# A row softmax on one core: the third tile loaded in eight DMAs of every eighth partition, and the split row of the second tile made whole

## The chip, the core and the metric

The kernel runs on one core of a Trainium2 chip. The core has five engines with their own instruction streams: TensorE (PE), VectorE (DVE), ScalarE (ACT), GpSimd (POOL) and SyncE (SP). Data moves between the chip's main memory (HBM) and the on-chip memory (SBUF, 128 partitions) in DMAs. A DMA is issued by SP, ACT or POOL into a queue of that engine, and is carried out in packets by the core's 16 DMA engines. Each DMA counts a semaphore up by 16 when it has landed, one by each DMA engine.

The metric is the device time of one execution in microseconds (us). Three runs of the kernel before gave 160.0, 160.11 and 161.32 us; the median is 160.11 us.

## The reference

```python
def setup_inputs():
    batch, seq, dim = 16, 1024, 512
    return {"x": np.random.randn(batch, seq, dim).astype(np.float32)}

def reference(x):
    x_scaled = x / 2.0
    x_max = np.max(x_scaled, axis=-1, keepdims=True)
    exp_x = np.exp(x_scaled - x_max)
    return (exp_x / np.sum(exp_x, axis=-1, keepdims=True)).astype(np.float32)
```

That is 16,384 rows of 512 fp32 values: 33.55 MB in, 33.55 MB out.

## The kernel before, in words

The 16,384 rows are laid out as 128 rows for each of the 128 partitions, 2 KB each. They are cut into ten tiles (`TILES`, L10): tile 0 has 3 rows per partition, tile 1 has 5, and tiles 2 to 9 have 15 each. In HBM the rows of one partition in one tile stand one behind the other, so a 15-row tile is 128 runs of 30,720 bytes. The tiles live in one array, `arena`, of 98 rows per partition; tiles 8 and 9 reuse the places of tiles 0 to 3 (`LATE`, L14).

**Loads.** `load` (L113) issues one DMA for a tile. For tile 1 (`SPREAD`, L20) it issues three: the first four rows of all partitions, the fifth row of partitions 0 to 125, and the fifth row of partitions 126 and 127. `early` (L153) puts the load of tile 0 on SP and that of tile 1 on ACT, at the very start of the program, ahead of the engines' other setup. `loads` (L157) then has ACT issue tiles 2 to 7, one DMA each. POOL issues tiles 8 and 9 (L176 to L179), once the exponentials of the first 83 rows are done and the stores that free their places have landed.

**Compute.** PE does next to nothing: it waits for each tile's load in turn and then releases ACT's chunks of that tile (L193 to L194; 48 counts for the split tile, 16 for the others). ACT loads its table (L200) and computes the exponential of one row per instruction with the row's sum beside it (L204 for tile 0, L271 in a loop of 5-row chunks). The maximum is left out here: the sums are checked at the end (L180 to L190), and a second, slow path with the maximum runs only when a sum is out of bounds. DVE takes reciprocals of the sums (L166) and multiplies (L169), up to 15 rows at a time.

**Stores.** SP waits for DVE and issues one store for each tile (`store`, L135, its DMA at L137), in order, into the same queue that held the load of tile 0. At the end SP waits for the last stores to land (L257).

So there are three DMA queues. In the profile q1 is SP's (the load of tile 0 and all ten stores), q10 is ACT's (tiles 1 to 7), q0 is POOL's (tiles 8 and 9).

Of the kernel before, what the change touches and what calls it, by code (L numbers as in the profile page):

```python
# [16 lines left out]
HEAD = [3]  # L17
E = 5

SPREAD = 1  # L20

TURN = 83

# [5 lines left out]
def kernel(  # L29
# [5 lines left out]
    nc = tc.nc  # L35
# [6 lines left out]
    xf = x.flatten_outer_dims()  # L42
    of = out.flatten_outer_dims()
    N, D = xf.shape
    P = nc.NUM_PARTITIONS
# [14 lines left out]
    tiles, base = [], 0  # L60
# [5 lines left out]
    def dram(ap, t):  # L66
        b, r, _ = tiles[t]
        return ap[b * P : (b + r) * P].rearrange("(p r) d -> p r d", r=r)

    def sb(t):  # L70
        _, r, at = tiles[t]
        return arena[:, at : at + r, :]
# [5 lines left out]
    owner = [max(t for t, (b, _, _) in enumerate(tiles) if b <= s) for s in starts]  # L78
# [12 lines left out]
    ld = [nc.alloc_semaphore(f"ld{t}") for t in range(len(tiles))]  # L91
# [4 lines left out]
    s_go = nc.alloc_semaphore("s_go")  # L96
# [13 lines left out]
    g_rec = nc.alloc_semaphore("g_rec")  # L110
    g_mul = nc.alloc_semaphore("g_mul")

    def load(eng, t):  # L113
        r = tiles[t][1]
        parts = [(0, P, 0, r)]
        if t == SPREAD:
            parts = [(0, P, 0, r - 1), (0, 126, r - 1, r), (126, P, r - 1, r)]
        for p, q, lo, hi in parts:
            eng.dma_start(  # L119
                out=sb(t)[p:q, lo:hi], in_=dram(xf, t)[p:q, lo:hi]  # L120
            ).then_inc(ld[t], 16)

    stored_by = {u: s_home[t] for t, us in LATE.items() for u in us}
    for t, (_, r, at) in enumerate(tiles):
# [26 lines left out]
            eng.reg_add(i, i, 1)  # L151

    def early():  # L153
        load(nc.sync, 0)
        load(nc.scalar, 1)

    def loads():  # L157
        for t in range(2, min(LATE)):
            load(nc.scalar, t)

    def program():

        for j, ks in enumerate(pairs):
# [3 lines left out]
                out=recip[:, b : b + c], in_=stats[:, b : b + c]  # L167
            )._wait_ge(s_exp, ks[-1] + 1).then_inc(s_rec, 1)
            nc.vector.tensor_mul(  # L169
                out=arena[:, a : a + c],  # L170
# [6 lines left out]
        for t, us in LATE.items():  # L177
# [3 lines left out]
            out=inside[:, :], in0=stats[:, :], scalar1=LO, scalar2=HI,  # L181
# [3 lines left out]
            out=inside[:, :], in0=inside[:, :], scalar=1.0, in1=stats[:, :],  # L185
# [3 lines left out]
            out=flag[:, :], in0=total[:, :], scalar1=float(N), scalar2=None, op0=Alu.is_ge,  # L189
# [1 line left out]


        for t in range(len(tiles)):  # L193
            nc.tensor.wait_ge(ld[t], 48 if t == SPREAD else 16).then_inc(s_go, owner.count(t))  # L194
        nc.tensor.wait_ge(s_ones, 1)
        nc.tensor.matmul(  # L196
            total[:, :], lhsT=count[:, :], rhs=ones[:, :], start=True, stop=True
# [3 lines left out]
        for k, c in enumerate(HEAD):  # L201
            take(nc.scalar, s_go, 1)
            for b in range(starts[k], starts[k] + c):
                ins = nc.scalar.activation(  # L204
                    out=arena[:, b], in_=arena[:, b], func=Exp, scale=0.5,
# [75 lines left out]
    entry.instructions = []  # L281
    nc.switch_bb("main", None)
    early()
    first = list(entry.instructions)
    at = next(k for k, i in enumerate(head) if type(i).__name__ == "InstDrain")
    entry.instructions = head[:at] + first + head[at:]
    act = []
    entry.instructions = list(entry.instructions) + [i for i in jumps if i not in act]
    nc.switch_body(here, parent=None, valid_engines=[i.engine for i in jumps])
    loads()  # L290
    program()


# [28 lines left out]
```

## Time and profile before

| what | value | from |
|---|---|---|
| runs | 160.0, 160.11, 161.32 us | the times |
| span of the profiled execution | 158.7 us | the page's first line |
| what lies around the span | 1.3 to 1.4 us | fastest run and median, less the span; the page has no other time of the profiled execution |
| busy: ACT, DVE, POOL, PE | 80.8, 73.2, 2.2, 0.2 us | the page, part 1 |
| DMA engines, all queues | 50.4 + 37.1 + 11.5 = 99.0% of 16 engines' span | the page, part 3 |
| bytes | 67.11 MB, mean 423 GB/s | the page |
| load of tile 0, issue to landing | 5.6 us | the page, part 6 |
| first exponential | at 6.96 us | the timeline |
| first exponential of tile 2 | at 17.71 us | the timeline |
| first store issued | at 10.94 us | the timeline of SP |
| loads of tiles 8 and 9 issued | at 87.70 us | the timeline of POOL |
| last store issued | at 143.66 us | the timeline |
| SP's wait for the last stores | 14.7 us | SP's waits |

How to read it: a busy share of an engine says what it did over the whole span, and none of the five is near full. The row called DMA in part 2 is the mean busy share of the 16 DMA engines in each fortieth of the span, and the row below it what they moved. In an answer for single stretches of time the last two figures are again the DMA share and the GB/s; a packet is counted there, whole, in the stretch in which it starts, so a short stretch can show more than 1.00.

### The profile page before, as it was taken

How to read it: one execution, taken by the hardware profiler on the slowest of the kernel's cores; microseconds unless marked ns; L12 is line 12 of the kernel's file. 1: busy time of each engine (PE TensorE's matmuls, PEld its weight loads, DVE VectorE, ACT ScalarE, POOL GpSimd, SP SyncE). 2: the span in 40 equal slices, each digit the busy share in tenths (PEclk: the TensorE clock that was granted, in tenths of full speed). 3: DMA queues.
4: the chain of work that ended last, by engine and by line, in shares of the span. 5: the costliest groups of instructions: out<-in, count | busy, mean ns of one | idle time of the engine just before them, and what ended most of it. 6: DMA issues, size and time to landing. Idle time of an engine off the chain costs nothing. (4 is left out here: it accounts for less than half of the span.)

```text
span 158.7 us, 657 instructions
## 1 busy us (share of the span) xinstructions
PE 0.2 (0%) x2; PEld 0.1 (0%) x2; DVE 73.2 (46%) x27; ACT 80.8 (51%) x257; POOL 2.2 (1%) x8
## 2 busy tenths in 40 slices
PE   0000000000000000000000000000000000000000
PEld 0000000000000000000000000000000000000000
DVE  0047001992981990059500991008932981992000
ACT  0590598697498008940399001991597009940000
POOL 0000000000000000000000300000000000010000
DMA  7999998989999999999999999999999999999995
GB/s 271 382 496 396 463 437 324 480 382 485 410 457 410 457 410 449 418 449 418 441 426 441 426 434 434 426 441 426 441 418 449 418 449 410 457 403 465 403 457 256
DMA packets 3024, 67.11 MB, mean 423 GB/s; under 512 B 336, under 2 KB 336, under 8 KB 720
## 3 DMA queue, kind: packets, MB, share of 16 engines
q1 hardware_dynamic: 1584, 34.34, 50.4%
q10 hardware_dynamic: 1152, 24.90, 37.1%
q0 software_dynamic: 288, 7.86, 11.5%
HBM read 33.55 MB, written 33.55 MB: 423 GB/s over the span
## 5 line engine op out<-in xcount | busy, mean ns | idle before, releaser
L271 ACT ACTIVATE arena<-arena x125 | 76.8, 615 | 54.1 <-ACTq L140 54.1
L169 DVE TENSOR_TENSOR arena<-arena,recip 128x7680 f32<-128x7680 f32 (+2 forms) x12 | 70.2, 5847 | 0.4
L166 DVE RECIPROCAL recip<-stats 128x15 f32<-128x15 f32 (+2 forms) x12 | 2.7, 224 | 70.4 <-ACT arena L271 61.4
L271 ACT ACTIVATION_READ_ACCUMULATOR arena<-arena x125 | 23.4, 187 | 0.0
L200 ACT ACT_TABLE_LOAD x1 | 1.3, 1283 | 5.7 <-issue 5.7
L119 POOL DMA_DIRECT2D arena<-in_x_dram x2 | 1.3, 638 | 84.9 <-ACT arena L271 84.9
L204 ACT ACTIVATE arena<-arena 128x512 f32<-128x512 f32 x3 | 1.9, 619 | 0.0
L180 POOL TENSOR_SCALAR inside<-stats 128x128 f32<-128x128 f32 x1 | 0.6, 630 | 51.7 <-ACT arena L271 51.7
L204 ACT ACTIVATION_READ_ACCUMULATOR arena<-arena 128x1 f32 x3 | 0.6, 188 | 0.0
L196 PE MATMUL total<-ones,count 128*1 128x1 f32 x2 | 0.2, 164 | 143.9 <-DVE inside L184 143.9
L184 DVE SCALAR_TENSOR_TENSOR inside<-inside,stats 128x128 f32<-128x128 f32 x1 | 0.3, 282 | 0.0
L188 DVE TENSOR_SCALAR flag<-total 1x1 int32<-1x1 f32 x1 | 0.1, 146 | 0.3 <-PE total L196 0.3
L196 PEld LDWEIGHTS total<-ones,count 128*1 128x1 f32 x2 | 0.1, 80 | 143.9 <-DVE inside L184 143.9
L175 POOL MEMSET ones<- 128x1 f32 x1 | 0.1, 98 | 2.2 <-POOLq L37 2.2
L306 POOL MEMSET const-bfloat16-1.0<- 128x1 bf16 x1 | 0.1, 108 | 0.0
L306 POOL MEMSET const-uint8-127<- 128x1 uint8 x1 | 0.1, 108 | 0.0
L306 POOL MEMSET const-float32-0.0<- 128x1 f32 x1 | 0.1, 104 | 0.2 <-issue 0.2
L306 POOL MEMSET const-float32-1.0<- 128x1 f32 x1 | 0.1, 104 | 0.0
L184 DVE DVE_READ_ACCUMULATOR inside<-inside,stats 128x1 f32 x1 | 0.1, 80 | 0.0
## 6 DMA issues: line engine op xcount, KB each, us to landing
out_dram<-arena SPq DMA_DIRECT2D x8, 3840.0 KB, 26.2
arena<-in_x_dram ACTq DMA_DIRECT2D x6, 3840.0 KB, 46.7
arena<-in_x_dram POOLq DMA_DIRECT2D x2, 3840.0 KB, 33.6
out_dram<-arena SPq DMA_DIRECT2D x1, 1280.0 KB, 22.9
arena<-in_x_dram ACTq DMA_DIRECT2D x1, 1024.0 KB
arena<-in_x_dram SPq DMA_DIRECT2D x1, 768.0 KB, 5.6
out_dram<-arena SPq DMA_DIRECT2D x1, 768.0 KB, 14.6
arena<-in_x_dram ACTq DMA_DIRECT2D x1, 252.0 KB
```

The lines of the kernel that those rows point to most:

```text
L119: eng.dma_start(out=sb(t)[p:q, lo:hi], in_=dram(xf, t)[p:q, lo:hi]).then_inc(ld[t], 16)
L166: nc.vector.reciprocal(out=recip[:, b : b + c], in_=stats[:, b : b + c])._wait_ge(s_exp, ks[-1] + 1).then_inc(s_rec, 1)
L169: nc.vector.tensor_mul(out=arena[:, a : a + c], in0=arena[:, a : a + c], in1=recip[:, b : b + c].unsqueeze(2).to_broadcast([P, c, D]),)._w ...
L175: nc.gpsimd.memset(ones[:, :], 1.0).then_inc(s_ones, 1)
L180: nc.gpsimd.tensor_scalar(out=inside[:, :], in0=stats[:, :], scalar1=LO, scalar2=HI, op0=Alu.max, op1=Alu.min,)._wait_ge(s_exp, len(sizes) ...
L184: nc.vector.scalar_tensor_tensor(out=inside[:, :], in0=inside[:, :], scalar=1.0, in1=stats[:, :], op0=Alu.mult, op1=Alu.is_equal, accum_ou ...
L188: nc.vector.tensor_scalar(out=flag[:, :], in0=total[:, :], scalar1=float(N), scalar2=None, op0=Alu.is_ge,)._wait_ge(s_tot, 1).then_inc(s_f ...
L196: nc.tensor.matmul(total[:, :], lhsT=count[:, :], rhs=ones[:, :], start=True, stop=True)._wait_ge(s_cnt, 2).then_inc(s_tot, 1)
L200: nc.scalar.preload_act_table(Exp)
L204: ins = nc.scalar.activation(out=arena[:, b], in_=arena[:, b], func=Exp, scale=0.5, accum_out=stats[:, b : b + 1],)
L271: ins = nc.scalar.activation(out=data, in_=data, func=Exp, scale=0.5, accum_out=stats[:, r : n_rows - E + 1 + r][:, bass.ds(now, 1)],)
L306: nc = _bacc.Bacc("TRN2", target_bir_lowering=False, num_devices=1)
```

## The change

The split of tile 1's fifth row goes: tile 1 is again one DMA of 128 partitions. Tile 2 is loaded in eight DMAs instead of one. DMA number g of the eight takes partitions g, g + 8, g + 16 and so on, 16 partitions with 30,720 bytes each. SP issues the first of them ahead of its load of tile 0; ACT issues the other seven behind tile 1, in front of tiles 3 to 7. All eight count the same semaphore, and PE waits for 128 counts in place of 16. Computation, stores and the late loads stay as they are.

```diff
-SPREAD = 1
+PRIMER = 2
+STEP = 8
...
-    def load(eng, t):
-        r = tiles[t][1]
-        parts = [(0, P, 0, r)]
-        if t == SPREAD:
-            parts = [(0, P, 0, r - 1), (0, 126, r - 1, r), (126, P, r - 1, r)]
-        for p, q, lo, hi in parts:
-            eng.dma_start(
-                out=sb(t)[p:q, lo:hi], in_=dram(xf, t)[p:q, lo:hi]
-            ).then_inc(ld[t], 16)
+    def load(eng, t, part=slice(0, P)):
+        eng.dma_start(out=sb(t)[part], in_=dram(xf, t)[part]).then_inc(ld[t], 16)
+
+    pieces = [slice(g, P, STEP) for g in range(STEP)]
...
     def early():
+        load(nc.sync, PRIMER, pieces[0])
         load(nc.sync, 0)
         load(nc.scalar, 1)
 
     def loads():
         for t in range(2, min(LATE)):
-            load(nc.scalar, t)
+            for part in pieces[1:] if t == PRIMER else [slice(0, P)]:
+                load(nc.scalar, t, part)
...
         for t in range(len(tiles)):
-            nc.tensor.wait_ge(ld[t], 48 if t == SPREAD else 16).then_inc(s_go, owner.count(t))
+            nc.tensor.wait_ge(ld[t], 16 * STEP if t == PRIMER else 16).then_inc(s_go, owner.count(t))
```

## The prediction

> **What bounds the kernel now.** I read the page's busy shares first, then its DMA rows, then what SP's queue waited for.
>
> ```profile
> span 158.7 us, 657 instructions
> ...
> PE 0.2 (0%) x2; PEld 0.1 (0%) x2; DVE 73.2 (46%) x27; ACT 80.8 (51%) x257; POOL 2.2 (1%) x8
> ...
> DMA  7999998989999999999999999999999999999995
> ```
>
> No compute engine is busy for more than 51% of the span, while the DMA engines are at nine tenths in all but the first, two early and the last slice. The queues' shares add up to 99.0%. So the time is the DMA engines' work, plus what they lose at the start, plus the tail.
>
> ```profile
> SPq L257 <- DMA out_dram<-arena: 14.7, 1, 14.7
> ```
>
> SP waits 14.7 us for stores after it has issued the last one, at 143.66 us. A whole 15-row store is eight packets on each engine; at 1.134 us each (below) that is 9.1 us. The remaining 5 us or so are queue still to be drained: compute may be up to 5 us later at the end and cost nothing. What counts is whatever makes the DMA engines stand still or move their bytes more slowly. For that I asked for short stretches at the start:
>
> ```profile
> 1.00:1.50 0.50, 0.00 (x0) 0.00 (x0) 0.00 (x0) 0.00 (x0) 0.00 (x0) 1.00 0.94 221
> 1.50:2.00 0.50, 0.00 (x0) 0.00 (x0) 0.00 (x0) 0.00 (x0) 0.00 (x0) 1.00 0.90 344
> ...
> 5.69:6.44 0.75, 0.00 (x0) 0.00 (x0) 0.00 (x0) 0.75 (x1) 0.00 (x0) 1.00 0.95 371
> 6.44:7.94 1.50, 0.00 (x0) 0.00 (x0) 0.00 (x0) 1.49 (x4) 0.00 (x0) 1.00 1.10 360
> 7.94:9.08 1.14, 0.00 (x0) 0.00 (x0) 0.14 (x1) 1.14 (x5) 0.00 (x0) 1.00 1.00 431
> 9.08:10.22 1.14, 0.00 (x0) 0.00 (x0) 1.10 (x2) 1.14 (x5) 0.00 (x0) 1.00 1.00 431
> ```
>
> The last two figures are DMA share and GB/s. The last two rows are one packet of tile 2 on each of 16 engines: 16 x 30,720 bytes in 1.14 us. The packet records give 1.134 us from start to start, 27.1 bytes per ns and engine. The first packets of tile 2, in the row 6.44 to 7.94, took 1.50 us: 0.36 us lost on every engine. They stand right behind the split row (5.69 to 6.44), the only load whose partitions are dealt out in nines, and not in eights. There the counts of the semaphore came late: 0.61 to 0.94 us after the engine's last packet (the trace's packet and counter records), against 0.29 to 0.54 us for every whole-tile store and load from tile 2 on. The two engines that carry nothing of the split row were still on their own 8 KB packets of the first four rows, and their counts came late too, by at least 0.55 us. I read this as writes into SBUF of different engines that got into each other's way: the plain deal by eights does not show it.
>
> **The change, part by part.**
>
> *The whole fifth row.* Two issues (0.67 and 0.24 us of ACT's queue) and their counts go. Each engine now writes 10,240 bytes in one packet (0.385 us, the 10 KB packets of tile 1's store) in place of 8,192 and 2,048 (0.309 + 0.084, each overlapping its neighbour by 0.004): some 0.005 us times eight, 0.04 us. If the 0.36 us are the split row's doing, they go as well; if they belong to the first big packet, they stay. Take half: -0.2. The row also let two engines carry 16 KB less (0.6 us); they gain it back as work, and this is next.
>
> *The first piece on SP.* It has 16 packets, one for each engine. In 1.5 to 2.0 us the share is 0.90, so 14.4 of 16 engines have work: two start about 0.9 us late. That is what the missing 16 KB made up for. With one packet per engine in front, all sixteen may start at 1.0 us: the two gain 0.9 and take 0.6 more. Averaged over 16 engines this is 0.1 us at best and zero if the start stays as it is; take -0.05.
>
> *SP's queue.* Tile 0 now stands behind 30,720 bytes per engine and shares the engines with tile 1 from the first packet: eight times (0.230 + 0.381) us, 4.9 us, after a packet of 1.13 to 2.27. It lands at 1.0 + 1.1 + 4.9 + 0.35 = 7.4 us, or 8.5 with the longer packet, where it took 5.6. The first exponentials move from 6.96 to at most 8.5 us, and the first store from 10.94 to 12.5. ACT's idle time before tile 2 hides that:
>
> ```profile
> 17.71 0.63 ACT L271 ACTIVATE arena<-arena  x1 [5.73 <-ACTq L140]
> ```
>
> There are 5.73 us to give, and loads keep the DMA engines busy meanwhile. Without this cover the 1.5 us would have to come out of the 5 us at the end, also free.
>
> *ACT's queue.* It issues 13 DMAs, not 9: one for tile 1 (0.39), seven pieces at 0.24 (the two-partition DMA) to 0.56 (the dearest whole tile), five whole tiles at 0.45 to 0.56. They started 1.17 us after the early ones ended; by the same step the pieces run from 1.7 to between 3.6 and 5.7 us, the tiles to 6.2 or 8.3, and the table load to 7.5 or 9.6 us. At worst tile 0 waits 1.1 us longer for ACT, under the same 5.73 us. The engines do not run dry: piece 0, tiles 0 and 1 keep each busy for 1.13 + 1.84 + 3.05 = 6.0 us from 1.0. PE's wait for 128 counts has tile 3 behind it on PE, whose load is queued behind the pieces anyway.
>
> *Counts.* Tile 1 has two fewer, tile 2 seven more; at 0.006 to 0.009 us on each engine +0.04 us.
>
> *The pieces' own packets.* Bytes and packet size stay: 8 x 1.134 = 9.07 us per engine if they run like the plain deal. But each piece has 16 engines write 16 partitions eight apart, a deal that the trace does not show. Bounds: nothing, by the 1.14 us rows, or twice the time if two engines meet at every packet, +9.07. The nearest row is the split row: 0.26 MB at 430 GB/s is 0.61 us, and 0.36 were lost, so 1.6 times as long; for eight packets +5.4. There the engines met by chance, nine partitions each and up to 0.4 us apart; in the pieces the pattern is the same for every engine and packet. So I take two on one. Less what stores hide: from 12.5 us an engine alternates a piece with a 6 KB store packet of 0.23 us, in which its partner has the way to itself; about five pieces are left by then (ACT's seven begin at 1.0 + 2.27 + 1.84 + 3.05 = 8.2 us, and (12.5 - 8.2) / 2.27 = 2 are done), so up to 1.2, say 0.6. And engines that are staggered by 0.2 us save that: 9.07 - 0.6 - 0.2 = +8.3. The DMA engines stay the bound afterwards and have no idle time to make it up with.
>
> [...]
>
> **Sum.** On the profiled 158.7 us: -0.04 - 0.2 - 0.05 + 0.04 + 8.3 = +8.05, span 166.7; with the 1.4 us by which the median of 160.11 stands over the span, 168.1 us.
>
> **The rivals.**
> 1. *No meeting (not slower).* A piece gives each engine one partition of the eight it has anyway, and every packet takes 1.14 us. For it: all sixteen engines moved whole tiles side by side at 431 GB/s, and the nine-partition packets themselves took 0.084 us almost to the last. It decides at the first packets of ACT's pieces, near 7 us: 1.1 us each, and the change gains 0.05 to 0.5 us at the start: 159.6 to 160.1, take 159.8.
> 2. *Some meeting.* As in the split row: +5.4, less 0.25: 165.3 us. For it the measured 1.6; against it that its stagger does not recur.
> 3. *The start doesn't change.* The last two engines start late in the short DMA too, and now carry 0.6 us more: +0.6 without meeting, 160.7, and it adds to the others. Against it: 32 packets with counts are far fewer than the 144 before.
> 4. *ACT's queue becomes the bound.* If a piece took ACT over 1.13 us to issue, the engines would run dry; at seven times 0.5 us more, 163.6. Its dearest issue so far is 0.67 us, which speaks against it.
>
> **How the numbers follow.** Two on one 0.45, some meeting 0.15, ACT's queue 0.02: slower by over 1% 0.62. Rivals 1 and 3 lie within 1%, which is about what three runs from 160.0 to 161.32 can tell from no change: 0.31 + 0.04 = 0.35. Faster by over 1% needs 1.6 us, and all that the start could give is 0.5: 0.03 for what I have not seen. The forecast is that of the likeliest case, 168.1. Its own range is 166.5 to 169.4 (all store cover and no cover, with 0.2 more at the top). The other sign holds 0.38, so the range must reach it: 159.7 to 169.4.
>
> **What would show it.** Right: stretches of 2.3 us for each round of 16 piece packets, about 217 GB/s at a DMA share of about 1, from 8 to 24 us; tile 2's first exponential near 25 us and not 17.71; POOL's loads and the last store about 8 us later; SP's last wait still near 14.7 us. Wrong: 431 GB/s in the same stretches and POOL's loads near 87.7 us; then the sum has lost its one large term. Gaps with a low share between 6 and 12 us would be rival 4.

## The result, and the profile after

The changed kernel takes 170.12 us (median of six runs, 169.7 to 170.82), the kernel before 160.0 us beside it. The ratio is 1.0631, with a 95% interval of 1.0596 to 1.0666: 10.1 us slower. The forecast was 168.1 us with a range up to 169.4, so the direction and most of the size were right and the time came out 0.7 us above the range. Some runs of the kernel before and of a few experiments were disturbed; the ratios leave them out.

The GB/s row of the page before, and the page of the changed kernel with the lines that answer to those shown before:

```profile
GB/s 271 382 496 396 463 437 324 480 382 485 410 457 410 457 410 449 418 449 418 441 426 441 426 434 434 426 441 426 441 418 449 418 449 410 457 403 465 403 457 256
```

```profile
span 169.2 us, 662 instructions
...
DMA  9999989999999999999999999999999999999995
GB/s 271 318 209 250 203 182 362 426 437 426 448 438 407 450 458 414 407 465 429 429 421 450 421 414 443 399 421 458 436 421 429 443 436 399 458 443 421 421 458 247
...
q1 hardware_dynamic: 1616, 34.83, 48.8%
q10 hardware_dynamic: 1088, 24.41, 39.1%
...
arena<-in_x_dram ACTq DMA_DIRECT2D x7, 480.0 KB, 16.4
...
arena<-in_x_dram SPq DMA_DIRECT2D x1, 768.0 KB, 17.5
```

The span grew by 10.5 us, from 158.7 to 169.2. The DMA engines are as busy as they were (nine tenths in all slices but the sixth and the last), but from the second to the sixth slice, 4.2 to 25.4 us, they move 182 to 318 GB/s. After that they move 362, and from then on 399 to 465 in all but the last slice, as before. Tile 0 lands 17.5 us after its issue; before it was 5.6. The packets of the seven pieces of tile 2 stand under ACT's 480 KB issues.

Short stretches of the same kernel show where that is (the last two figures are DMA share and GB/s; a packet counts where it starts):

```profile
1.10:1.60 0.50, 0.00 (x0) 0.00 (x0) 0.00 (x0) 0.00 (x0) 0.00 (x0) 1.00 1.04 205
1.60:2.10 0.50, 0.00 (x0) 0.00 (x0) 0.00 (x0) 0.00 (x0) 0.00 (x0) 1.00 0.73 205
...
3.20:4.84 1.64, 0.00 (x0) 0.00 (x0) 0.00 (x0) 0.00 (x0) 0.00 (x0) 1.00 1.23 325
4.84:8.11 3.27, 0.00 (x0) 0.00 (x0) 0.00 (x0) 0.00 (x0) 0.00 (x0) 1.00 0.88 298
8.11:10.88 2.77, 0.00 (x0) 0.00 (x0) 0.00 (x0) 1.28 (x1) 0.00 (x0) 1.00 1.03 248
...
18.15:20.55 2.40, 0.00 (x0) 0.00 (x0) 0.21 (x2) 2.22 (x7) 0.00 (x0) 1.00 1.00 205
20.55:22.93 2.38, 0.00 (x0) 0.00 (x0) 1.73 (x1) 2.38 (x9) 0.00 (x0) 1.00 1.01 207
22.93:25.34 2.41, 0.00 (x0) 0.00 (x0) 1.94 (x2) 0.41 (x2) 0.00 (x0) 1.00 0.99 204
...
27.32:28.46 1.14, 0.00 (x0) 0.00 (x0) 0.00 (x0) 0.48 (x1) 0.00 (x0) 1.00 1.04 447
```

In each of the rows from 18.15 to 25.34 us sixteen packets of 30,720 bytes take 2.4 us at a share of 1.00: every engine is busy, and all of them are half as quick as on a plain load (1.138 us a packet). The row of 27.32 us is a stretch of tile 3, a plain load: 447 GB/s, full rate again. The two rows from 3.20 to 8.11 us hold SP's piece, whose packets all start in the first of them, and none of ACT's; together they move 307 GB/s only ((325 x 1.64 + 298 x 3.27) / 4.91). And the engines are not all up any earlier than before: by the packet records 9 or 10 packets are under way from 1.4 to 1.8 us, where the kernel before had 14; in both it is 16 by 2.2 us.

SP's last wait, from the list of waits:

```profile
SPq L255 <- DMA out_dram<-arena: 16.9, 1, 16.9
```

It was 14.7 us. SP's queue has more left to drain at the end than before, so the time was not lost in compute.

The sum over the trace's packet records agrees. For each packet I took its duration less that of an undisturbed packet of its size (30,720 bytes 1.138 us, 10,240 bytes 0.385, 8,192 bytes 0.309, 6,144 bytes 0.234), added these up, and divided by 16 engines:

| us lost per engine | before | after | all pieces by ACT |
|---|---|---|---|
| packets of tile 2's pieces | – | 8.62 | 8.67 |
| tile 0 | 0.25 | 0.81 | 0.36 |
| tile 1 | 0.14 | 0.94 | 0.09 |
| other 30 KB packets up to 30 us | 0.85 | 0.59 | 0.03 |
| 30 KB packets after 30 us | 0.08 | 0.48 | 0.06 |
| tile 0's store | 0.00 | 0.00 | 0.44 |
| sum | 1.32 | 11.44 | 9.65 |

The rows add up to 10.1 us more than before, of 10.5 in the span; the first packet at 1.17 and not 1.00 us is another 0.2. (In "before", tile 2 itself is under the other 30 KB packets. The third column is an experiment below; its rows add up to 8.3 us more than before, of 8.4 in its span.)

### The profile page after: what moved, and what is told of

Its sections match the earlier page's. It is cut to its first block, busy times and chain, and to the rows that moved or that the text cites. A ratio compares the mean times of both kernels' runs of the same rounds, so it can differ in the third digit from the quotient of the medians.

```text
span 169.2 us, 662 instructions
## 1 busy us (share of the span) xinstructions
PE 0.2 (0%) x2; PEld 0.1 (0%) x2; DVE 73.2 (43%) x27; ACT 80.6 (48%) x257; POOL 2.2 (1%) x8
## 6 DMA issues: line engine op xcount, KB each, us to landing
arena<-in_x_dram SPq DMA_DIRECT2D x1, 768.0 KB, 17.5
out_dram<-arena SPq DMA_DIRECT2D x1, 768.0 KB, 16.9
```

## The experiments

Theory A, a guess taken from the split row: engines that write certain sets of partitions of SBUF get in each other's way; where two packets of 30,720 bytes then take about twice the 1.138 us, their engines are said to meet. Theory B: a DMA with one packet per engine is slow in itself, whatever its partitions are. Theory C: it is the rows in HBM, 240 KB apart from engine to engine, that are slow to read. The first line of each diff names the kernel that the run differs from, "before", "after" or an experiment.

### Tile 1 whole, tile 2 whole

```diff
 before
-        parts = [(0, P, 0, r)]
-        if t == SPREAD:
-            parts = [(0, P, 0, r - 1), (0, 126, r - 1, r), (126, P, r - 1, r)]
+        parts = [(0, P, 0, r)]
...
-            nc.tensor.wait_ge(ld[t], 48 if t == SPREAD else 16).then_inc(s_go, owner.count(t))
+            nc.tensor.wait_ge(ld[t], 16).then_inc(s_go, owner.count(t))
```

> The kernel before with tile 1 loaded by one DMA; tile 2 stays one DMA. Theory A (engines that write crowded partitions share a way into SBUF): the split row's nines are gone, so tile 2's first packets take 1.14 us and not 1.50 (-0.36 us), but the two engines that start late carry 0.6 us more: 160.0 to 160.7 us. Theory B (DMAs with one packet per engine are slow in themselves) and theory C (rows of HBM eight apart are slow to read) say nothing of it: 160.0 to 160.7 us for the late start alone, with tile 2's first packets at 1.50 us if that belongs to the first large packet.

Measured: ratio to the kernel before 1.0017 (1.0002 to 1.0032). It was run again:

> The kernel with tiles 1 and 2 whole once more, since three of its six runs were disturbed: 160.0 to 160.4 us. Its profile shows whether tile 2's first packets take 1.14 or 1.50 us without the split row in front of them; with the small load ahead of tile 0 they took 1.14.

Measured: ratio 1.0048 (1.0033 to 1.0063). So the whole row costs 0.3 to 0.8 us, where I had it as a gain of 0.24. In the second run's packet records the first sixteen packets of tile 2 take 1.138 us each, not 1.50. But its seventh round, from 13.2 us, takes 1.35 to 1.76 us, and in the first 30 us its packets of all sizes lose 1.24 us per engine, against 1.23 before: the loss has moved, not gone. What this run loses more, 0.5 us, stands in 30 KB packets after 30 us (0.58 against 0.08), where the two kernels are the same. In the profiles of the changed kernel and of the versions below these late packets lose 0.04 to 0.98 us, with and without pieces; the cause is open, and with it that of the 0.3 to 0.8 us.

### All eight pieces by ACT

```diff
 after
-    pieces = [slice(g, P, STEP) for g in range(STEP)]
+    pieces = [slice(g, P, 8) for g in range(8)]
...
     def early():
-        load(nc.sync, PRIMER, pieces[0])
         load(nc.sync, 0)
         load(nc.scalar, 1)
 
     def loads():
         for t in range(2, min(LATE)):
-            for part in pieces[1:] if t == PRIMER else [slice(0, P)]:
+            for part in pieces if t == PRIMER else [slice(0, P)]:
...
-            nc.tensor.wait_ge(ld[t], 16 * STEP if t == PRIMER else 16).then_inc(s_go, owner.count(t))
+            nc.tensor.wait_ge(ld[t], 16 * len(pieces) if t == PRIMER else 16).then_inc(s_go, owner.count(t))
```

> Tile 1 whole, tile 2 in eight DMAs of every eighth partition, all eight issued by ACT; SP loads tile 0 first, as before. All theories: tile 2's packets take 2.2 to 2.4 us and the time is 168 to 170.5 us. If the place of the first DMA ahead of tile 0 cost anything of its own, this is faster than the changed kernel by that much: tile 0 lands at 5.6 us and not at 17.5, stores start near 12 us and can hide up to 1.2 us; 168.5 to 169.5. If the place costs nothing: 170.

Measured: 168.47 us, ratio 1.0533 (1.0519 to 1.0547). The pieces alone, over the kernel with whole tiles (1.0017 to 1.0048), cost 4.8 to 5.2%, 7.8 to 8.3 us. Their packets lose 8.67 us per engine, the same as in the changed kernel. What SP's part adds is 1.0631 - 1.0533, 1.6 us (1.0 to 2.2 by the two intervals).

The store of tile 0 started here at 20.8 us, among the last pieces. Its 6 KB packets took up to 0.49 us in place of 0.234 and lost 0.44 us per engine: a packet that runs beside a piece is slowed as well.

### Tile 2 in two halves

```diff
 all pieces by ACT
-    pieces = [slice(g, P, 8) for g in range(8)]
+    pieces = [slice(0, 64), slice(64, P)]
```

> Tile 1 whole, tile 2 in two DMAs, partitions 0 to 63 and 64 to 127, four packets on each engine in each. [...] Theory B: four packets per engine and DMA, next to no loss, 160 to 161 us. Theory C: neighbouring rows, no loss, 160 to 161 us.

Measured: 168.61 us, in one run. The stretches while tile 2 is loaded, first two of the kernel before, then three of this one:

```profile
8.00:10.00 2.00, 0.00 (x0) 0.00 (x0) 1.02 (x2) 2.00 (x8) 0.00 (x0) 1.00 1.03 445
10.00:12.00 2.00, 0.00 (x0) 0.00 (x0) 0.91 (x1) 1.98 (x8) 0.00 (x0) 1.00 1.14 492
```

```profile
8.00:10.00 2.00, 0.00 (x0) 0.00 (x0) 1.18 (x2) 2.00 (x9) 0.00 (x0) 1.00 1.05 215
10.00:12.00 2.00, 0.00 (x0) 0.00 (x0) 0.91 (x2) 1.81 (x6) 0.00 (x0) 1.00 1.05 215
12.00:14.00 2.00, 0.00 (x0) 0.00 (x0) 1.97 (x2) 0.00 (x0) 0.00 (x0) 1.00 1.20 246
```

The kernel before moved 445 and 492 GB/s from 8 to 12 us. Here it is 215. These are 64 neighbouring partitions, with neighbouring rows in HBM and four packets per engine; most packets of the first half take 2.40 us, most of the second 1.9 to 2.2. Tile 2's packets lose 8.12 us per engine and those after 30 us 0.23, so the added time lies in this load. Theory B and theory C both said no loss: they fall.

### Every seventh partition

```diff
 all pieces by ACT
-    pieces = [slice(g, P, 8) for g in range(8)]
+    pieces = [slice(g, 112, 7) for g in range(7)] + [slice(112, P)]
```

> Tile 1 whole, tile 2 in seven DMAs of every seventh partition of the first 112 and one of partitions 112 to 127. [...] Theory B: as the changed kernel, 2.3 us for every packet, 169 to 170.5 us. Theory C: seven apart reads like eight apart, 2 us and more for the seven, the last one 1.14 us: 168 to 169.5 us.

Measured: 167.42 us in one run, below what theories B and C expected. In the second, third and seventh round nearly all packets took 2.0 to 2.2 us, in the others mostly 1.4 to 2.0. The packets of the last DMA, sixteen neighbours, took 2.8 to 3.7. Why nearly all packets are slow in three of the rounds is not shown by any run.

### What sets of partitions cost by themselves

Two probes load sets of partitions into the place of tiles that are loaded again later, ahead of everything else. The first takes one DMA at a time:

```diff
 tiles 1 and 2 whole
     def early():
+        bench, rows = sb(7), dram(xf, 7)
...
+        nc.sync.dma_start(out=bench[0:2:1], in_=rows[0:2:1]).then_inc(s_probe, 16); nc.sync.wait_ge(s_probe, 32)
...
+        nc.sync.dma_start(out=bench[0:121:8], in_=rows[0:16:1]).then_inc(s_probe, 16); nc.sync.wait_ge(s_probe, 304)
...
+        nc.scalar.wait_ge(s_probe, 352)
         load(nc.sync, 0)
```

> Ahead of everything else, 22 loads of tile 7's rows into its place, one at a time, each waited for (the rows are loaded again later, so nothing is left out; the span is longer by the probes). Each is a set of partitions, first with engines 0 and 1 alone: partition 0 and 1, 0 and 2, 0 and 4, 8, 16, 32, 64; then 16 partitions in steps of 1 to 8; then 64 neighbours, every second of 128, 16 by eight in SBUF from neighbouring rows and the other way round, 126, 128. [...] Theory B (a DMA with one packet per engine is slow): all pairs and all sixteens alike. Theory C: the slow ones go with the rows in HBM and not with the partitions.

Measured, from the packet records (first packet's start to last packet's end): sixteen neighbours 4.21 us, in steps of 2 to 8 2.77, 3.73, 2.81, 2.67, 2.73, 2.40 and 2.86. The step of 3 stands out among the steps, and the neighbours take longest. Sixteen by eight from neighbouring rows of HBM took 2.80 against 2.86, sixteen neighbours from rows eight apart 4.43 against 4.21. So it goes with the partitions in SBUF, and theory C falls once more. The pairs told nothing: a single first packet of an idle engine takes 1.2 to 2.4 us anyway, its latency included, and that hides who meets whom. And 126 partitions, in nines, took 11.54 us for nine packets, with a median of 1.138 us: no crowding.

The second probe gives each engine four packets in a row:

```diff
 tiles 1 and 2 whole
     def early():
...
+        [nc.sync.dma_start(out=sb(t)[0:33:32], in_=dram(xf, t)[0:33:32]).then_inc(s_probe, 16) for t in (4, 5, 6, 7)]; nc.sync.wait_ge(s_probe, 448)
...
```

> Ahead of everything else, for each of 17 sets of partitions four loads back to back (rows of tiles 4 to 7, loaded again later), then a wait: so that each engine has four packets in a row and the second to fourth are free of the first one's latency. Sets: partition 0 alone; 0 with 1, 2, 4, 8, 16, 32, 64; four in steps of 1, 4, 8 and 32; 16 in steps of 8 and 4; 32 in steps of 1 and 4; 64 in steps of 2. [...]

The stretches of this run (last figure GB/s): partitions 0 and 1; 0 and 4; 0 and 32; 0 and 64; four neighbours; four in steps of 4; sixteen in steps of 8; 32 in steps of 4:

```profile
7.50:17.20 9.70, 0.00 (x0) 0.00 (x0) 0.00 (x0) 0.00 (x0) 0.00 (x0) 1.00 0.12 25
...
31.20:36.80 5.60, 0.00 (x0) 0.00 (x0) 0.00 (x0) 0.00 (x0) 0.00 (x0) 1.00 0.11 44
...
52.60:61.50 8.90, 0.00 (x0) 0.00 (x0) 0.00 (x0) 0.00 (x0) 0.00 (x0) 1.00 0.12 28
63.20:68.70 5.50, 0.00 (x0) 0.00 (x0) 0.00 (x0) 0.00 (x0) 0.00 (x0) 1.00 0.12 45
69.80:87.60 17.80, 0.00 (x0) 0.00 (x0) 0.00 (x0) 0.00 (x0) 0.00 (x0) 1.00 0.24 28
90.20:95.80 5.60, 0.00 (x0) 0.00 (x0) 0.00 (x0) 0.00 (x0) 0.00 (x0) 1.00 0.24 88
...
116.20:126.50 10.30, 0.00 (x0) 0.00 (x0) 0.00 (x0) 0.00 (x0) 0.00 (x0) 1.00 0.91 191
...
161.80:172.20 10.40, 0.00 (x0) 0.00 (x0) 0.00 (x0) 0.00 (x0) 0.00 (x0) 1.00 0.93 378
```

Two engines together move 25 to 28 GB/s on partitions 0 and 1 or 0 and 32, about what one engine moves alone once it is under way (30,720 bytes in 1.138 us, 27 GB/s), and 44 to 45 on 0 and 4 or 0 and 64. Four neighbours move 28, four in steps of 4 move 88. In microseconds a packet, once under way:

| partitions | us a packet | against 0 alone |
|---|---|---|
| 0 alone | 1.138 | 1 |
| 0 and 1; 0 and 2; 0 and 32 | 2.41; 2.39; 2.15 to 2.29 | 2.1; 2.1; 1.9 to 2.0 times |
| 0 and 4; 0 and 16; 0 and 64 | 1.138 | 1 |
| 0 and 8 | 1.32 to 1.41, then 1.138 | 1.2, then 1 |
| 0, 1, 2, 3 | 4.5 to 4.8 | 4.0 to 4.2 times |
| 0, 4, 8, 12; 0, 8, 16, 24 | 1.138 | 1 |
| 0, 32, 64, 96 | 2.2 to 2.4 | 1.9 to 2.1 times |
| 16 in steps of 8; 16 in steps of 4; 32 neighbours | 2.40 (medians) | 2.1 times |
| 32 in steps of 4; 64 in steps of 2 | 1.138 (medians) | 1 |

So theory A stands for the sets tried: partition 0 meets 1, 2 and 32 (2.15 to 2.41 us) and does not meet 4, 16 and 64 (1.138). The middle packets of 0 and 8, at 1.32 to 1.41 us, stay open. Both sixteens hold 0 and 32 and take 2.40 us; 32 in steps of 4 holds them too and takes 1.138. Why, and what the partitions that meet have in common, no run here shows.

### The same change with steps of four, and of two

```diff
 after
-STEP = 8
+STEP = 4
```

> The changed kernel with one number changed, STEP = 4 for 8: tile 2 in four DMAs of 32 partitions four apart, the first on SP ahead of tile 0. [...] Theory B (few packets per engine): two per engine, about half the loss, 164 to 166 us.

Measured: 160.26 us, ratio 1.0017 (1.0005 to 1.0029). The stretches in which tile 2 is loaded:

```profile
8.00:10.00 2.00, 0.00 (x0) 0.00 (x0) 0.00 (x0) 0.01 (x1) 0.00 (x0) 1.00 1.08 458
10.00:12.00 2.00, 0.00 (x0) 0.00 (x0) 0.00 (x0) 0.00 (x0) 0.00 (x0) 1.00 1.19 510
12.00:14.00 2.00, 0.00 (x0) 0.00 (x0) 0.00 (x0) 1.40 (x5) 0.00 (x0) 1.00 1.04 445
```

Full rate, with the first piece still on SP ahead of tile 0. The 96 packets of ACT's three pieces take 1.138 us each; SP's first sixteen, which now start at 1.33 us on idle engines and ahead of ACT's, 1.72 on average. One number in the source takes away 9.8 of the 10.1 us. Theory B, with about half the loss, falls once more.

> The changed kernel with STEP = 2: two DMAs of every second partition, the first on SP ahead of tile 0. The probe gave 1.14 us a packet for such a DMA alone, so no meeting: 159.9 to 160.6 us. SP's first packet near 3 us again if a strided DMA is slow to set up.

With STEP = 2 in the same place: ratio 1.003 (1.0015 to 1.0045), 160.47 us, inside the expected 159.9 to 160.6.

### Where SP's part comes from

```diff
 after
     def early():
-        load(nc.sync, PRIMER, pieces[0])
         load(nc.sync, 0)
+        load(nc.sync, PRIMER, pieces[0])
         load(nc.scalar, 1)
```

> The changed kernel with the order of SP's two loads turned round: tile 0 first, then the first piece of tile 2. If the piece's place ahead of tile 0 is what costs 1.6 us over the version with all pieces on ACT (168.47), this gives 168.2 to 168.8 us, with SP's first packet near 1.0 us and tile 0 landed by 6 to 7 us. If it is SP's taking part at all, 169.5 to 170.2 us.

Measured: 169.15 us, ratio 1.0564 (1.0538 to 1.059), between the two expectations. Of SP's 1.6 us, 1.1 come from the place ahead of tile 0 (1.0631 - 1.0564) and 0.5 from SP's taking part at all (1.0564 - 1.0533); the intervals of the last two ratios touch (1.0538 to 1.059, 1.0519 to 1.0547), so the 0.5 is not clear of noise. In this run SP's first packet starts at 1.0 us; in the changed kernel it starts at 3.2 us, and ACT's tile 1 goes first.

```diff
 tiles 1 and 2 whole
+    first = nc.alloc_sbuf_tensor("first", (P, D), fp32)
...
     def early():
+        nc.sync.dma_start(
+            out=first[0:P:8, :], in_=dram(xf, 2)[0:P:8, 0, 0:D]
+        ).then_inc(s_first, 16)
         load(nc.sync, 0)
...
+        nc.sync.wait_ge(s_first, 16)
```

> Tile 1 and tile 2 whole; ahead of tile 0 SP issues one small load of 16 partitions eight apart, 2 KB each, into a place that nothing reads. If a DMA with one packet per engine brings all engines up early: 16 engines busy from 1.0 us, 0.1 to 0.4 us faster than the kernel with whole tiles, 159.7 to 160.1. If instead the small DMA holds SP's queue back as in the changed kernel (first packet at 3.2 us, ACT's tile 1 first): tile 0 lands 1 to 2 us later, the engines start on tile 1, and the time is 160.0 to 160.6, within 0.3 us of whole tiles without it, because nothing meets and the delay is covered.

Measured: 160.02 us, ratio 1.0005 (0.9996 to 1.0014). Again SP's first packet comes late, at 3.6 us, and ACT's tile 1 goes first, at 1.14. Tile 1's packets, now the first on idle engines, lose 0.61 us per engine, nearly all before 3.2 us, and tile 0's behind them nothing. The first store is late as well:

```profile
17.66 119.74 SPq L134 DMA_DIRECT2D out_dram<-arena  x10
```

That is 6.7 us later than the 10.94 of the kernel before, and the time is the same. So a store this late costs nothing here, where tile 2 is not in pieces. The same small load in front of the kernel before, with its split row:

```diff
 before
+    first = nc.alloc_sbuf_tensor("first", (P, D), fp32)
...
     def early():
+        nc.sync.dma_start(
+            out=first[0:P:8, :], in_=dram(xf, 2)[0:P:8, 0, 0:D]
+        ).then_inc(s_first, 16)
         load(nc.sync, 0)
...
+        nc.sync.wait_ge(s_first, 16)
```

> The kernel before, its row split kept, with the small load of 16 partitions (2 KB each, into a place that nothing reads) ahead of tile 0 on SP. With whole tiles this load made up for what the whole row cost: 160.02 against 160.2 to 160.8. If it brings the late engines up, the split row now gives them too little to do, and the time is 160.0 to 160.4; if it helps by something else, the two add up and this is 0.2 to 0.5 us faster than the kernel before, 159.4 to 159.8, and faster than both kernels.

Measured: 160.76 us, ratio 1.0063 (1.0042 to 1.0084), slower than either expectation. With whole rows the small load made up for what the whole row cost, with the split one it harms; no run here shows why. None of these versions beats the kernel before.

## Why the prediction was right in its cause and short in its size

**What bounds the kernel.** Right. The DMA engines stayed busy throughout, SP's last wait did not shrink (16.9 against 14.7 us), and the loss at the start came through to the end whole.

**The pieces' own packets.** Right that the packets take about twice as long, and near in size partly by luck. The term was +8.3; the records give 8.62, and the runs 7.8 to 8.3. Rounds of 2.4 us at 205 GB/s stand where 2.3 us and 217 were to show it, tile 2's first exponential came at 27.98 us, and POOL's loads were issued at 96.64, 8.9 us later. But two errors cancelled in part. Two engines that meet take 2.39 us a packet and not 2.27: eight such packets lose 10.0 us, not 9.07. And 1.4 of that came back, not 0.8, and not from stores: the first store was issued at 22.3 us and its first packet started at 27.9, behind the last piece. It came back where pieces ran beside shorter packets, in SP's piece (1.91 us a packet) and in the four rounds of ACT's that alternated with tile 0 (2.09 to 2.21). Nor is such cover free, as the term had it: the covering packets are slowed themselves (tile 0's lost 0.81 us per engine). That two engines meet in every packet was a choice between two bounds that no row then decided; the probes (2.40 us a packet for sixteen partitions eight apart), the halves (2.40 us for most of the first) and STEP = 4 (1.138 us) bear out the twofold time, and with them the rivals "no meeting" and "some meeting" fall.

**The evidence for it.** Half wrong. I read the split row's late counts and the 1.50 us behind it as writes that meet. The probe's 126 partitions in nines ran at 1.138 us a packet, so nines do not crowd in 30 KB packets, and with a whole row in its place the stretch turned up elsewhere (13.2 us). The counts were late, but by what is open. The conclusion held because of the 2.40 us that the probes show for sixteen partitions eight apart, not because of that row, and the factor of 1.6 taken from it measured nothing of the kind.

**The whole row.** I put it at -0.24 us; the runs say +0.3 to +0.8 (1.0017 and 1.0048). The 0.2 us from the 1.50 us stretch did not come: that stretch went, and another of the same size stood at 13.2 us. Why the whole row costs anything is open, as told above.

**The first piece and SP's queue.** This is the step that failed. I had it at -0.05 us, with tile 0 landing at 8.5 us at the latest under ACT's idle time, free. It cost 1.6 us, most of the 2.0 by which the sum fell short. The whole row and the pieces together make up the other 0.4 (8.5 us in the kernel with all pieces by ACT, where I had 8.1 with the counts). Two things were wrong in it. The first piece didn't come first: its first packet started at 3.2 us, and by then ACT's tile 1 was running. And the sum slowed the pieces' own packets alone; for the packets that run beside a piece it had nothing. So the piece met tile 1's packets, which is the 307 GB/s from 3.20 to 8.11 us: from 4.84 us on they lost 0.53 us per engine, where those of the kernel with the small load lost 0.05 after 3.2 us. With SP's two loads turned round, where the piece starts at 5.25 us among them, they lost 0.61 there. (The other 0.41 of tile 1's 0.94 was lost before the piece's first packet, by packets on idle engines, as in the kernel with the small load, where it cost no time.) Tile 0, third in line, alternated packet by packet with ACT's pieces and lost 0.81, where behind the small load it lost nothing. With steps of four the same two tiles lost 0.02 and 0.00. Tile 0 landed 17.5 us after its issue:

```profile
9.25 1.28 ACT L198 ACT_TABLE_LOAD   x1 [9.25 <-issue]
18.33 0.63 ACT L202 ACTIVATE arena<-arena 128x512 f32<-128x512 f32 x1 [7.80 <-ACTq L136]
```

The table was loaded by 10.5 us and ACT then stood still for 7.8 us until tile 0 was there. That lateness in itself is free, as far as the small load shows it (first store at 17.66 us, ratio 1.0005); what costs is that packets of other tiles run beside pieces and are slowed (tile 0's by 0.81 us per engine, tile 1's by 0.53 from 4.84 us on). Against the kernel with all pieces by ACT the table above gives SP's part as +0.85 (tile 1), +0.45 (tile 0), +0.56 (other early 30 KB packets), +0.42 (later ones, of which I have no cause), -0.05 (the pieces) and -0.44 us (tile 0's store, which met pieces there and not here), 1.8 in all. With 0.15 for the later first packet that is 1.9 us, of 2.1 between the two profiled spans and 1.6 between the ratios.

**ACT's queue.** Its 13 DMAs took until 9.2 us and the table load until 10.5, where I had at most 9.6: a piece costs 0.56 to 0.61 us to issue. It was covered, by tile 0's own lateness. From 2.2 to 27 us at least 15 packets were under way at any time, so the engines didn't run dry and this rival falls.

**The start unchanged.** That rival was right in its first half: the engines came up later, not earlier (9 or 10 packets under way from 1.4 to 1.8 us, against 14). Its price of 0.6 us is of the size of what the whole row costs, but the records of that run put the loss after 30 us, so its second half is not shown.

**The range.** Its ends do not follow from the terms that it names. All store cover gives 167.5 us, no cover and no stagger 168.9, and 169.1 with 0.2 more, not 166.5 and 169.4. The measured time lies above all of these, because the term that failed had no room for a loss.

## What to carry to other kernels

Probe a slice of partitions by itself before slicing a load by partitions: here sixteen partitions eight apart take 2.40 us a packet, 32 four apart 1.138, and the one number between them is worth 9.8 us of 160. The pieces slowed what ran beside them too (tile 0's packets lost 0.81 us per engine), so add the neighbours' packets to the sum. And issue order was not arrival order (the first piece, issued at 0.0 us, started its packets at 3.2, behind ACT's at 1.17): look for the first packet of each queue, not for the first issue.

## What the runs showed that I had not expected

- Two engines on partitions 0 and 1 or 0 and 2 take 2.39 to 2.41 us for a packet that takes one engine 1.138, 5% more than double (0 and 32 took 2.15 to 2.29). Four on 0 to 3 take 4.5 to 4.8, about four times.
- 32 partitions in steps of 4 run at full rate although they are a quarter of the 128 (1.138 us a packet), while 64 neighbours run at about half the rate (2.40 for most packets of the first half, 1.9 to 2.2 of the second). The size of a set did not tell its rate.
- A DMA of 16 partitions eight apart as SP's first instruction starts its packets at 3.2 to 3.6 us, behind ACT's load that was issued 0.12 us later and starts at 1.14 to 1.17; a load of 128 partitions in the same place starts at 1.00, one of 32 partitions four apart at 1.33, and one of 64 partitions two apart at 2.66, again behind ACT's. This is left open.
- In sevens nearly all packets took 2.0 to 2.2 us in three of the seven rounds, and mostly 1.4 to 2.0 in the others. This is left open too.
